# A fused two-block transformer on one core: where the last products of a gated block, the pooling bands and the pooling tiles stand, and which engine multiplies the post-norm vectors of channels 512 up

## The chip, the core and the metric

The kernel runs on one core of a Trainium2 chip. Five engines work at once, each through its own queue in the order of that queue: TensorE (PE in the profile, its weight loads PEld), VectorE (DVE), ScalarE (ACT), GpSimd (POOL), and SyncE (SP), which issues the transfers. Semaphores hold an instruction until its inputs are there; what stands behind a held instruction on the same engine waits too. The metric is the device time of one execution in microseconds.

## The reference, cut to what is computed

512 tokens of 1024 channels in float32 pass through two blocks. The first (modulated norms, a gating and convolution mixer, a gated feed-forward) is not touched. The second has two layers, an attention layer and a pooling layer, each with a gated feed-forward behind it:

```python
def second_block(h, g, ...):
    for layer in range(2):
        u = rmsnorm(h, g[layer][0])
        m = mixer_fox_nsa(u, ...) if layer == 0 else mixer_pool(u, ...)
        h = h + rmsnorm(m, g[layer][1])          # post-norm of the mixer
        u = rmsnorm(h, g[layer][2])
        h = h + rmsnorm(swiglu(u, ...), g[layer][3])   # post-norm of the feed-forward

def mixer_pool(h, w_groups, scale):      # four groups of 256 channels, windows 2, 4, 8, 16
    mean = trailing mean of the group's window of tokens
    pooled = mean - h                    # per group
    return einsum('bsgc,gcd->bsgd', pooled, w_groups) * scale
```

So four post-norms stand in the second block: attention, first gated block, pooling, second gated block. The trailing mean reaches at most 15 tokens back, so a tile of 128 tokens needs itself and the tile before it.

## The kernel before

**Tiles.** The residual `XT` is token-major: four tiles `i` of 128 tokens, each in two halves `j` of 512 channels. A product keeps float32 by three passes over operands split into a high and a low part (`wh`, `wl` of weights, `H` or `hid` of activations). A weight is loaded raw by SP, copied to `wh` on ScalarE and subtracted to `wl` on VectorE; `W.ahead(n)` asks for `n` such splits ahead of use. All engine instructions are recorded through one helper, so they carry one line, L113 before and L111 after; the tile names tell them apart.

**A post-norm** (`PostT`) has, for each token tile, per half: the mixer's or feed-forward's result is put into `mg` on VectorE (out of PSUM), `square` sums its squares on ScalarE (`sq<-mg`) and multiplies `mg` in place by the norm's vector `gb`. `TG[j]` says whether GpSimd (True) or VectorE (False) does this. `close` makes the root (`sd` on VectorE, its square root on ScalarE, the reciprocal `rs` on VectorE) and adds `mg*rs` to `XT` (two instructions `XT<-mg,rs,XT`), with two squares on ScalarE. `to_raw` then transposes `XT` on TensorE in eight products (`ax<-fixed,XT`) and puts each into `H`, high part on ScalarE, low part on VectorE: the input of the next gated block.

**First gated block** (`f2`). `front` computes all but the last 6 of the 22 hidden slabs of the down product into `mg`. `f2.last(h, j)` does the last 6 slabs for token tiles 2h and 2h+1 and half j: 18 products `mm<-wh,hid` and `mm<-wl,hid` of 128x512 for each tile, 36 in all. Behind `last(h, 1)` comes, per tile, `after2`: `close`, then `to_pool`, which writes the scaled tile as `xs` (half 0 on ScalarE, half 1 on VectorE).

**Pooling.** `band(c0, c1)` makes the pooled input of 256 tokens with banded matrices: for each of 8 channel slices it multiplies `xs` by a band (`ax<-bf,xs` and `ax<-bm,xs`, two or three products) and puts the result into `H`, 128x256, high part on ScalarE and low part on VectorE. `pool_step(i)` multiplies the four groups of tile i by their maps (48 products `mm<-wh,H` and `mm<-wl,H` for two tiles, 24 each), evacuates with `mg<-mm,gb` and does `square`, `close` and `to_raw` of the pooling post-norm.

**Second gated block** (`f3`). A "head" is one slab of 128 hidden channels, gate and up, on tokens 0 to 255: 48 products `mm<-H,wh` and `mm<-H,wl` of 128x256. There are five heads ahead of the block's `front`. Two of them, `HN3[0]`, were emitted with `late`, which holds their evacuation back.

**The order.** A scheduler places instructions on each engine's queue from program order as priority and from its own estimate of when inputs are ready; the queues are then fixed. The main sequence of the pooling layer (lines 1735 to 1754) sets the priorities; L113 is the helper `g`.

Of the kernel before, what the change touches and what calls it, by code (L numbers as in the profile page):

```python
# [32 lines left out]
HALVES = ((0, 256), (256, 512))  # L33
# [37 lines left out]
HEAD = 3  # L71
HEAD2 = 3
HEAD3 = 5
HN3 = (2, 0)
HN = (2, 1)
HNP = 8
POOLX = (2, 6)
# [15 lines left out]
B2 = ()  # L93
NB2 = 8
TAGS.update({n: ("b2", NB2) for n in B2})
LATE = 1
KEEPF = ()
KEEP = True
KEEPS = False
TG = (True, True)  # L100


class Ordered:
# [17 lines left out]
def body(ctx: ExitStack, tc: tile.TileContext, I: dict, out, dbg=None):  # L121
# [19 lines left out]
    def SQ():  # L141
        return tp.tile([P, S], F32, tag="sq", name="sq", bufs=BS)
# [13 lines left out]
    def AXP():  # L156
        return ps.tile([P, S], F32, tag="ax", name="ax", bufs=2)

    def act(o, i, f=AF.Identity, **kw):
        ins = SC.activation(o, i, f, **kw)  # L160
        if f in KEEPF and not SC.on:
            tc.keep_in_program_order(ins)
        return ins
# [269 lines left out]
    def drain(it):  # L433
        deque(it, maxlen=0)
# [453 lines left out]
    for h in range(8):  # L888
        hp, e = divmod(h, 2)
# [45 lines left out]
    def heads(n, **kw):  # L935

        for _ in range(min(n, len(nx["head"]))):
            nx["head"].popleft()(**kw)
# [80 lines left out]
    class PostT:  # L1019
# [13 lines left out]
        def square(self, i, j):  # L1033
            mv = self.m(i, j)
            act(SQ(), mv, AF.Square, accum_out=self.ss[:, i, j:j + 1])
            (G if TG[j] else V).tensor_tensor(mv, mv, self.gb[:, j], op=OP.mult)

# [606 lines left out]
    f2 = FfnT(HO, raw0, HEAD2)  # L1644
# [47 lines left out]
    def band(c0, c1):  # L1692
        i0 = c0 // P

        def xk(i, k):
            return xs[i][:, k // 4, (k % 4) * P:(k % 4 + 1) * P]

        for k in range(KD):
            lv = k // 2
            bm = bands["m"][:, lv]  # L1700
            o = AXP()[:, :HS]
            TE.matmul(o, lhsT=xk(i0, k), rhs=(bm if c0 else bands["f"][:, lv]), start=True, stop=False)
            TE.matmul(o[:, P:], lhsT=xk(i0 + 1, k), rhs=bm[:, :P], start=False, stop=(c0 == 0))
            if c0:
                TE.matmul(o[:, :16], lhsT=xk(i0 - 1, k), rhs=bm[:, P:P + 16], start=False, stop=True)
            HO.put(k, o, c0, c1, scale=ng2[:, 1, 0, k:k + 1])
# [3 lines left out]
    def pool_step(i):  # L1710
        psb, pp = pf["psb"], pf["pp"]
        for j in range(2):
            (wh, wl, _), = getp(j)
            o = MM()
            for e in range(2):
                g = 2 * j + e
                mm_tok(o[:, e * HS:(e + 1) * HS], HO, [(wh[:, 2 * e:2 * e + 2], wl[:, 2 * e:2 * e + 2], 2)], i, 2 * g)
            tt(pp.m(i, j), o, psb[:, j], OP.mult)
            pp.square(i, j)
        pp.close(i)  # L1720
        pp.to_raw(i)
# [13 lines left out]
    f2.last(0, 0)  # L1735
    f2.last(0, 1, after2)
    f2.last(1, 0)
    band(*HALVES[0])
    pool_step(0)
    pool_step(1)  # L1740
    f2.last(1, 1, after2)
    f3 = FfnT(HO, raw1, HEAD3)
    W.ahead(6)
    late = []
    heads(HN3[0], late=late)
    band(*HALVES[1])
    if LATE:
        drain(e() for e in late)
    heads(HN3[1])
    if not LATE:  # L1750
        drain(e() for e in late)
    pool_step(2)
    pool_step(3)
    heads(HEAD3)
# [26 lines left out]
```

## Time and profile before

| | us |
|---|---|
| median of 3 runs (1666.96, 1671.49, 1671.66) | 1671.49 |
| profiled execution | 1667.07 |
| span of the profiled execution, first to last instruction | 1665.3 |
| TensorE busy in it | 1627.4 |
| VectorE, ScalarE, GpSimd busy | 881.8, 681.8, 129.5 |

The profiled execution lies 4.4 us under the median. Its page gives the busy time of each engine, the chain of work that ended last, and the granted TensorE clock; the answers on its trace give, in order of time, what each engine did, how long it stood idle, and what released it. In the span's times, the stretch that the change rearranges runs from 1253.5 (end of the products of `last(1, 0)`) to 1304.7 us (end of the products of `pool_step(3)`). Before, TensorE does in it: band 0 with steps 0 and 1, `last(1, 1)` with the transposes of tiles 0 and 1 set among its products, two heads, band 1 with steps 2 and 3.

### The profile page before, as it was taken

How to read it: one execution, taken by the hardware profiler on the slowest of the kernel's cores; microseconds unless marked ns; L12 is line 12 of the kernel's file. 1: busy time of each engine (PE TensorE's matmuls, PEld its weight loads, DVE VectorE, ACT ScalarE, POOL GpSimd, SP SyncE). 2: the span in 40 equal slices, each digit the busy share in tenths (PEclk: the TensorE clock that was granted, in tenths of full speed). 3: DMA queues.
4: the chain of work that ended last, by engine and by line, in shares of the span. 5: the costliest groups of instructions: out<-in, count | busy, mean ns of one | idle time of the engine just before them, and what ended most of it. 6: DMA issues, size and time to landing. Idle time of an engine off the chain costs nothing.

```text
span 1665.3 us, 22096 instructions
## 1 busy us (share of the span) xinstructions
PE 1627.4 (98%) x8797; PEld 1358.9 (82%) x8797; DVE 881.8 (53%) x1645; ACT 681.8 (41%) x1232; POOL 129.5 (8%) x144
## 2 busy tenths in 40 slices
PE   7999899999999999999999999999999999999998
PEld 5776698887888998777778988888888998888886
DVE  5799585444333584678857344423257734432144
ACT  4585352222222364455658233213237823232232
POOL 0452000000000001100001000000013100000002
PEclk9999999999999999999999999999999999999999
DMA  9635435544531423311144232234134232232411
GB/s 306 179 111 193 152 112 175 154 149 133 153 101 54 120 57 90 90 26 52 39 107 124 61 111 61 95 114 144 59 102 114 77 89 77 83 121 93 121 64 51
DMA packets 245168, 179.55 MB, mean 108 GB/s; under 512 B 20688, under 2 KB 220224, under 8 KB 245064
## 3 DMA queue, kind: packets, MB, share of 16 engines
q1 hardware_dynamic: 240520, 176.99, 36.3%
q10 hardware_dynamic: 4544, 1.14, 0.4%
q8 instruction: 69, 1.13, 0.3%
q14 instruction: 35, 0.29, 0.1%
HBM read 175.99 MB, written 2.11 MB: 107 GB/s over the span
## 4 chain that ended last, share of the span: by engine, by line
PE 86%; DVE 3%; ACT 2%; issue 0%; DMA 0%; SPq 0%; DVEq 0%; ACTq 0%
PE mm L113 79%; PE ax L113 4%; PE st L113 3%; DVE pw L113 1%; ACT sq L113 0%; DMA raw<-in_w_out_dram 0%; ACT pw L113 0%; DVE XT L113 0%; DVE wl L113 0%; DVE sq L113 0%; ACT wh L113 0%; ACT H L113 0%; DVE pt L113 0%; DVE fk L113 0%; DVE mg L113 0%
## 5 line engine op out<-in xcount | busy, mean ns | idle before, releaser
L113 PE MATMUL mm<-H,wh 128*128 128x512 f32 (+1 forms) x3168 | 869.8, 361 | 9.2 <-ACT wh L113 3.4
L113 PEld LDWEIGHTS mm<-H,wh 128*128 128x128 f32 x3168 | 564.1, 189 | 104.5 <-issue 4.4
L113 PE MATMUL mm<-H,wl 128*128 128x512 f32 (+1 forms) x1584 | 567.7, 359 | 2.9 <-DVE wl L113 2.9
L113 DVE TENSOR_TENSOR wl<-raw,wh 128x1024 fp32r<-128x1024 f32 (+1 forms) x257 | 310.4, 1223 | 217.0 <-ACT wh L113 203.2
L113 PEld LDWEIGHTS mm<-H,wl 128*128 128x128 f32 x1584 | 299.3, 189 | 47.7 <-DVE wl L113 3.5
L113 ACT ACTIVATE wh<-raw 128x1024 fp32r<-128x1024 f32 (+1 forms) x257 | 262.5, 1041 | 127.3 <-PE mm L113 52.8
L113 PE MATMUL mm<-wh,hid 128*128 128x512 f32 x704 | 217.3, 389 | 0.0
L113 DVE TENSOR_TENSOR silu<-silu,mm 128x512 f32<-128x512 f32 (+1 forms) x77 | 47.0, 611 | 250.0 <-PE mm L113 243.5
L113 PEld LDWEIGHTS mm<-wh,hid 128*128 128x128 f32 x704 | 132.1, 188 | 27.1
L113 ACT ACTIVATE hid<-silu 128x512 fp32r<-128x512 f32 (+1 forms) x77 | 43.8, 569 | 242.5 <-DVE silu L113 234.9
L113 PE MATMUL mm<-wl,hid 128*128 128x512 f32 x352 | 137.3, 390 | 0.0
L113 PE MATMUL mm<-hid,wh 128*128 128x512 f32 (+1 forms) x464 | 116.4, 340 | 0.0
L113 PEld LDWEIGHTS mm<-hid,wh 128*128 128x128 f32 x464 | 80.3, 190 | 9.9 <-issue 0.4
L113 POOL TENSOR_TENSOR mg<-mg,gb 128x512 f32<-128x512 f32 x32 | 44.3, 1389 | 464.6 <-ACT sq L113 456.0
L113 ACT ACTIVATE silu<-silu 128x512 f32<-128x512 f32 (+1 forms) x52 | 29.3, 565 | 123.1 <-DVE silu L113 123.0
L113 PE MATMUL mm<-hid,wl 128*128 128x512 f32 (+1 forms) x232 | 79.1, 341 | 0.0
L113 PEld LDWEIGHTS mm<-wl,hid 128*128 128x128 f32 x352 | 66.1, 188 | 14.0 <-DVE wl L113 0.3
L113 DVE TENSOR_TENSOR silu<-mm,rsb 128x512 f32<-128x512 f32 (+1 forms) x52 | 31.6, 608 | 73.0 <-PE mm L113 72.5
L113 PE MATMUL mm<-wh,H 128*128 128x512 f32 (+2 forms) x256 | 67.0, 350 | 1.6 <-ACT wh L113 1.6
L113 DVE TENSOR_TENSOR hid<-silu,hid 128x512 fp32r<-128x512 f32 (+1 forms) x77 | 47.3, 614 | 37.4 <-ACT hid L113 37.3
L113 POOL TENSOR_TENSOR cv<-cv,tap 128x488 f32<-128x488 f32 (+12 forms) x40 | 52.5, 1348 | 88.2 <-ACT cv L113 71.2
L113 ACT ACTIVATE silu<-mm 128x512 f32<-128x512 f32 (+1 forms) x25 | 13.7, 546 | 108.7 <-PE mm L113 108.7
(271 smaller groups left out, 1624.7 us busy)
## 6 DMA issues: line engine op xcount, KB each, us to landing
adaw<-in_ada_w_dram SPq DMA_DIRECT2D x48, 512.0 KB
raw<-in_w_ffn_in_dram SPq DMA_DIRECT2D x44, 512.0 KB
raw<-in_ffn_w_gate_dram SPq DMA_DIRECT2D x44, 512.0 KB
raw<-in_ffn_w_up_dram SPq DMA_DIRECT2D x44, 512.0 KB
raw<-in_ffn_w_down_dram SPq DMA_DIRECT2D x44, 512.0 KB
raw<-in_w_in_dram SPq DMA_DIRECT2D x16, 512.0 KB
adaw<-in_ada_f_w_dram SPq DMA_DIRECT2D x16, 512.0 KB
raw<-in_attn_w_in_dram SPq DMA_DIRECT2D x16, 512.0 KB
```

The lines of the kernel that those rows point to most:

```text
L113: ins = f(*a, **k)
```

## The change

`HN3` and `LATE` go. `f2.last(1, 1)` moves ahead of band 0, so all of the first gated block's last products precede both bands. Band 1 follows pooling steps 0 and 1; then come the construction of `f3`, `W.ahead(6)`, steps 2 and 3, and all five heads together. `TG` becomes `(True, False)`: the in-place product with the post-norm vector for channels 512 up goes to VectorE in every post-norm of the second block, 16 of the 32 instructions `mg<-mg,gb`.

```diff
-HN3 = (2, 0)
-LATE = 1
-TG = (True, True)
+TG = (True, False)
...
     f2.last(0, 1, after2)
     f2.last(1, 0)
+    f2.last(1, 1, after2)
     band(*HALVES[0])
     pool_step(0)
     pool_step(1)
-    f2.last(1, 1, after2)
+    band(*HALVES[1])
     f3 = FfnT(HO, raw1, HEAD3)
     W.ahead(6)
-    late = []
-    heads(HN3[0], late=late)
-    band(*HALVES[1])
-    if LATE:
-        drain(e() for e in late)
-    heads(HN3[1])
-    if not LATE:
-        drain(e() for e in late)
     pool_step(2)
     pool_step(3)
     heads(HEAD3)
```

**TensorE behind the products of pooling step 1.** Before, the last products of `last(1, 1)` stand there, with the transposes of tile 0 among them:

```order
L113 MATMUL mm<-wh,H_97 128x256 x2
L113 MATMUL mm<-wl,H_97 128x256
L113 MATMUL mm<-wh,hid 128x512 x2
L113 MATMUL mm<-wl,hid 128x512
L113 MATMUL mm<-wh,hid 128x512
L113 MATMUL ax<-fixed,XT 128x128 x4
L113 MATMUL mm<-wh,hid 128x512
L113 MATMUL ax<-fixed,XT 128x128 x4
L113 MATMUL mm<-wl,hid 128x512
```

After, the transposes stand there by themselves, nine, one small product, seven, and band 1 stands behind them:

```order
L111 MATMUL mm<-wh,H_97 128x256 x2
L111 MATMUL mm<-wl,H_97 128x256
L111 MATMUL ax<-fixed,XT 128x128 x9
L111 MATMUL st<-fixed 128x128
L111 MATMUL ax<-fixed,XT 128x128 x7
L111 MATMUL ax<-bm,xs 128x256
L111 MATMUL ax<-bm,xs 128x128
L111 MATMUL ax<-bm,xs 128x16
L111 MATMUL mm<-wh,H_90 128x256
L111 MATMUL ax<-bm,xs 128x256
```

What moved is `last(1, 1)`, now in front of band 0; all sixteen transposes of tiles 0 and 1 follow step 1 directly, and every product of band 1 is behind them.

**VectorE from the last put of band 0 to the residual of tile 0.** `wl` is a weight split, `mg<-mm,gb` the evacuation of a pooling product, `XT<-mg,rs,XT` the residual that the transposes wait for. Before:

```order
L113 SCALAR_TENSOR_TENSOR H_97<-ax,fixed,H_97 128x256
L113 TENSOR_TENSOR mg<-mm,gb 128x512 x2
L113 TENSOR_TENSOR wl<-raw,wh 128x1024
L113 TENSOR_TENSOR sd<-fixed 128x1
L113 TENSOR_TENSOR mg<-mm,gb 128x512
L113 RECIPROCAL rs<-sd 128x1
L113 SCALAR_TENSOR_TENSOR XT<-mg,rs,XT 128x512 x2
```

After:

```order
L111 SCALAR_TENSOR_TENSOR H_97<-ax,fixed,H_97 128x256
L111 RECIPROCAL rs<-sd 128x1
L111 TENSOR_SCALAR xs<-XT,rs 128x512
L111 TENSOR_TENSOR wl<-raw,wh 128x1024 x3
L111 TENSOR_TENSOR mg<-mm,gb 128x512 x2
L111 TENSOR_TENSOR wl<-raw,wh 128x1024
L111 TENSOR_TENSOR mg<-mm,gb 128x512
L111 TENSOR_TENSOR mg<-mg,gb 128x512
L111 TENSOR_TENSOR sd<-fixed 128x1
L111 TENSOR_TENSOR mg<-mm,gb 128x512
L111 RECIPROCAL rs<-sd 128x1
L111 TENSOR_TENSOR wl<-raw,wh 128x1024
L111 SCALAR_TENSOR_TENSOR XT<-mg,rs,XT 128x512 x2
```

Behind the last put there is now the `xs` of tile 3, then three splits in a row ahead of the first evacuation, one more between the evacuations of tiles 0 and 1, and one ahead of tile 0's residual; ScalarE's queue has the `wh` copies of the same weights there, four in a row. The three splits stood among the band's puts before, ahead of the first evacuation; a fourth stood behind it. One of tile 1's two evacuations stood ahead of tile 0's residual before; now both do, and a product `mg<-mg,gb` too.

**VectorE at the end of the program**, the post-norm of the last tile's channels 512 up. Before:

```order
L113 TENSOR_TENSOR mg<-mg,mm 128x512
L113 TENSOR_TENSOR sd<-fixed 128x1
L113 RECIPROCAL rs<-sd 128x1
L113 TENSOR_TENSOR rs<-rs,fixed 128x1
L113 SCALAR_TENSOR_TENSOR XT<-mg,rs,XT 128x512 x2
```

After:

```order
L111 TENSOR_TENSOR mg<-mg,mm 128x512
L111 TENSOR_TENSOR mg<-mg,gb 128x512
L111 TENSOR_TENSOR sd<-fixed 128x1
L111 RECIPROCAL rs<-sd 128x1
L111 TENSOR_TENSOR rs<-rs,fixed 128x1
L111 SCALAR_TENSOR_TENSOR XT<-mg,rs,XT 128x512 x2
```

The product with the vector stands on VectorE between the last addition to `mg` and the root; before it stood on GpSimd. In the other three post-norms it enters in the same way; the attention's post-norm is the third place where TensorE's order differs (the transposes of `XT` stand elsewhere among the output products).

## Rows read from the trace of the kernel before

**Rows 1.** the page: busy time by engine, and the chain that ended last

```profile
PE 1627.4 (98%) x8797; PEld 1358.9 (82%) x8797; DVE 881.8 (53%) x1645; ACT 681.8 (41%) x1232; POOL 129.5 (8%) x144
...
PE 86%; DVE 3%; ACT 2%; issue 0%; DMA 0%; SPq 0%; DVEq 0%; ACTq 0%
```

**Rows 2.** TensorE in time order: start, us, instruction, count, [idle before <-releaser]

```profile
1252.79 0.61 PE L113 MATMUL mm<-wh,hid 128*128 128x512 f32 x2
1253.24 0.39 PE L113 MATMUL mm<-wl,hid 128*128 128x512 f32 x1
1253.47 1.46 PE L113 MATMUL ax<-bf,xs 128*128 128x256 f32 x6
1256.93 1.42 PE L113 MATMUL ax<-bm,xs 128*128 128x128 f32 x6 [2.00 <-ACT xs L113]
...
1262.21 0.60 PE L113 MATMUL ax<-bf,xs 128*128 128x256 f32 x2
...
1262.86 0.60 PE L113 MATMUL ax<-bf,xs 128*128 128x256 f32 x2
...
1265.55 0.40 PE L113 MATMUL mm<-wh,H 128*128 128x256 f32 x2
...
1268.43 0.63 PE L113 MATMUL mm<-wh,hid 128*128 128x512 f32 x2
...
1270.66 0.63 PE L113 MATMUL ax<-fixed,XT 128*128 128x128 f32 x4 [1.14 <-DVE XT L113]
...
1280.02 0.40 PE L113 MATMUL mm<-H,wh 128*128 128x256 f32 x2
...
1291.89 4.46 PE L113 MATMUL ax<-bm,xs 128*128 128x256 f32 x30
...
1304.68 0.40 PE L113 MATMUL mm<-H,wh 128*128 128x256 f32 x2
```

**Rows 3.** windows of 2 us: busy by engine, then granted clock, DMA share, GB/s

```profile
1256.00:1258.00 2.00, 1.07 (x6) 1.10 (x6) 0.83 (x2) 1.94 (x4) 1.72 (x2) 0.79 0.49 143
1258.00:1260.00 2.00, 2.00 (x8) 1.73 (x8) 2.00 (x4) 1.17 (x4) 0.00 (x0) 0.50 1.16 315
1260.00:1262.00 2.00, 2.00 (x14) 1.81 (x13) 1.39 (x3) 1.99 (x4) 0.00 (x0) 0.86 1.16 290
```

**Rows 4.** VectorE in time order, same stretch

```profile
1257.76 1.22 DVE L113 TENSOR_TENSOR wl<-raw,wh 128x1024 fp32r<-128x1024 f32 x1 [1.17 <-ACT wh L113]
1258.90 1.26 DVE L113 SCALAR_TENSOR_TENSOR H<-ax,fixed,H 128x256 fp32r<-128x256 f32 x3
...
1265.02 1.43 DVE L113 TENSOR_TENSOR mg<-mm,gb 128x512 f32<-128x512 f32 x2
...
1279.20 0.61 DVE L113 SCALAR_TENSOR_TENSOR H<-ax,fixed,H 128x128 fp32r<-128x128 f32 x2
```

**Rows 5.** ScalarE in time order, same stretch

```profile
1250.44 0.72 ACT L113 ACTIVATE xs<-XT,rs 128x512 f32<-128x512 f32 x1 [0.30 <-DVE rs L113]
...
1256.69 1.04 ACT L113 ACTIVATE wh<-raw 128x1024 fp32r<-128x1024 f32 x1
```

**Rows 6.** waits of TensorE between 862 and 918 us

```profile
PE ax L113 <- DVE XT L113: 0.2, 1, 0.2
```

**Rows 7.** all engines in time order at the end

```profile
1657.45 0.39 PE L113 MATMUL mm<-wl,hid 128*128 128x512 f32 x1
...
1658.05 0.68 DVE L113 TENSOR_TENSOR mg<-mg,mm 128x512 f32<-128x512 f32 x1
...
1659.56 1.26 POOL L113 TENSOR_TENSOR mg<-mg,gb 128x512 f32<-128x512 f32 x1 [2.96 <-ACT sq L113]
...
1660.33 0.51 DVE L113 TENSOR_TENSOR rs<-rs,fixed 128x1 f32<-128x1 f32 x1
1660.88 1.42 DVE L113 SCALAR_TENSOR_TENSOR XT<-mg,rs,XT 128x512 f32<-128x512 f32 x2
```

**Rows 8.** VectorE in time order, some 20 us before the end

```profile
1640.85 0.16 DVE L113 TENSOR_TENSOR rs<-rs,fixed 128x1 f32<-128x1 f32 x1
```

## The prediction

> **What bounds the kernel now.** I read the page first: TensorE is busy 98% of the span and makes 86% of the chain that ended last [rows 1]. So a microsecond that TensorE waits is a microsecond of the kernel, and one of another engine counts only where TensorE then waits for it. Next I read TensorE in order of time where the change works [rows 2]. Two waits stand there: 2.00 us behind the first bands, until ScalarE has written the last `xs` of tile 1, and 1.14 us until VectorE has written `XT` of tile 0. Behind the first the granted clock falls: in 2 us windows 0.79, 0.50 and 0.86 [rows 3]. Full speed is 1.00, and 0.50 is the lower level (1.2 of 2.4 GHz), so the low time is 2 x (0.21 + 0.50 + 0.14)/0.50 = 3.4 us, and half of it, 1.7 us, is lost. From 1280.02 to 1304.68 no row shows a wait. The reader should see what covers the close of each pooling tile (evacuation, squares, root, residual, before TensorE can transpose): the 36 products of `last(1, 1)`, 8.2 us of work that needs nothing from it.
>
> **The change, the move of the last products.** I follow the queue of after with durations of before, from a common start at 1253.47, where `last(1, 0)` ends.
>
> Step 1. `last(1, 1)` now comes at once: 36 products, three in 0.68 us (1252.79 to 1253.47, [rows 2]), 8.2 us, to 1261.6. The `xs` of tile 1 are written meanwhile, so the 2.00 us wait, its 1.7 us of low clock and the 1.14 us wait go: 4.8 us.
>
> Step 2. Band 0 costs 0.65 us a slice (1262.21 to 1262.86, [rows 2]), eight make 5.2; step 0's 24 products at 0.12 us (step 1 takes 1265.55 to 1268.43) make 2.9: 1269.7. But the band's puts into `H` now share VectorE with the closes of tiles 2 and 3 of the first gated block: 8 puts of 0.42, a `mg` addition and a vector product of 0.7 each, two residuals of 0.7 [rows 4, 7], an `xs` at about 0.7 (as ScalarE's, [rows 5]) and six short ones of 0.16 [rows 8], in all 7.9 us, and some 1.5 us for which it waits on ScalarE's squares and roots between. From 1261.6 this ends the last put at about 1271.0. Step 0 then ends at 1271.2 (1.5 us lost) and step 1 at 1274.1.
>
> Step 3. Now the transposes of tile 0 stand next in TensorE's queue, and nothing is in front of them. VectorE's queue from 1271.0: three splits, paced by ScalarE's root (some 0.3), `xs` (0.7) and three copies (1.04 each), with a last `wl` of 1.22 [rows 4, 5]: 5.3 us, to 1276.3. Then two evacuations, a split, an evacuation, the product with the vector, the sum for the root, an evacuation while ScalarE makes the root, the reciprocal, a fifth split and the first half of tile 0's residual: six of 0.7, two of 1.2 and two of 0.16 make 6.9 us, less some 0.4, since an instruction in a row starts about 0.08 before the one ahead ends (1258.90 behind 1257.76 + 1.22, [rows 4]). TensorE gets it at 1282.8 and has waited 8.7 us. The five splits alone are 5 x 1.2 = 6 us of this.
>
> Step 4. Tile 1. Behind tile 0's residual stand a sixth split (1.2), eight low puts of 0.3 that alternate with ScalarE's high puts, a vector product (0.7), roots and the two residuals: 5.1 us of work besides the split, and some 1.3 us on ScalarE. That ends at 1291.0; the last transposes at 1291.4. From 1274.1 to there TensorE has 1.5 us of work, so it waits 15.8 us.
>
> Step 5. Band 1 with steps 2 and 3 is the same work as before, 1291.89 to 1304.68, 12.8 us. Its first products after the band wait for puts that now stand behind those of tile 1 on ScalarE and VectorE: from their queue I put 1.9 us. The clock: the 2.00 us wait above cost 1.7 us of low clock, and this wait is longer, so it costs that at least; I take 1.7, the row it is nearest to. If it stayed low through all of band 1 and steps 2 and 3, it would cost 12.8. End: 1291.4 + 12.8 + 1.9 + 1.7 = 1307.8.
>
> Step 6. The two heads that stood at 1280.02 to 1291.89, 11.9 us, now come behind: 1319.7, where before had done the same work at 1304.68. The transposes of tiles 2 and 3 stand among the heads' products, five times 48 at 0.12 us, some 29 us of other work, and cost no wait. The rest of TensorE's queue is as before. So the move costs **15.0 us**.
>
> **The vector product on VectorE.** 16 products of about 0.7 us (the `mg` evacuation, [rows 4]) leave GpSimd, where one takes 1.26 [rows 7]. In the pooling tiles they are in the sum. In the attention's post-norm TensorE waits 0.2 us in 56 us [rows 6]; with a product of 0.7 for each of four tiles ahead of roots that transposes wait for, it can grow by 1.5 at most if two such delays show, or by nothing; I take 0.5. At the second gated block all closes but the last lie beside products. At the end of the program the chain from the last product (1657.84) to the residual (1662.30) is 4.46 us and nothing covers it [rows 7]: the product adds 0.7. But the small `rs` product takes 0.51 us while GpSimd runs and 0.16 where it does not [rows 7, 8], so 0.35 comes back: +0.3, with 0 and 0.7 as bounds. By these rows an instruction of VectorE that meets one of GpSimd is the longer for it.
> The Trainium skill's Perfetto Trace Analysis, Optimizing Scalar/DVE Operations, says that GpSimd and VectorE share a read port, so that moving work between the two might not help. By that alone the move to VectorE would be worth nothing at the end instead of +0.3; the trace agrees that they hinder each other, and the order puts the product on the chain all the same.
>
> **The rivals.** *Short closes.* The splits may hardly hold VectorE, because their weights arrived early and they fit into its pauses during band 0. Then each close is as short as at the end of the program: 4.46 us from the last product. Step 0 ends at 1271.2, so tile 0's residual is there at 1275.7; step 1 ends at 1274.1, tile 1's at 1278.6, transposes to 1279.0. That is 12.4 us less than step 4's 1291.4, and the sum is 15.0 - 12.4 + 0.8 = +3.4: 1675, no change that can be told. For it: before, the first three splits do lie among the band's puts. Against it: in the new order they stand behind the last put and the `xs`, and a queue doesn't reorder; the three ahead of the evacuations and two behind are 6 us. It decides at about 10 us taken out of steps 3 and 4.
>
> *The removed waits win.* If besides the puts of step 2 and the `H` of step 5 came in time (1.5 and 1.9 us less), and the short waits left the clock high (1.7 less), the sum were 3.4 - 5.1 = -1.7, and with tile 1's close as well beside tile 0's transposes at most -5: 1666 to 1670, on the other side. The place is TensorE's wait behind step 1, the price 8.7 and 7 us in the forecast; it decides where both closes together show under 3 us. The 4.46 us at the end, with nothing else on VectorE, speaks against it.
>
> *Slower still.* The clock stays low through band 1 and steps 2 and 3: up to 11.1 more than in step 5, +27: 1698. For it: there are two waits, of 8.7 and 7 us, with few products between, four times the one that made the clock fall before. Against it: after that one the clock was full again within 3.4 us of low time [rows 3]. Late weights would act in the same way: in 1258 to 1262 the transfers run at 290 to 315 GB/s [rows 3], so 3 MB of loads take 10 us, and copies that wait for them hold VectorE's splits and all behind them.
> The Trainium skill's TensorE: Matmul & The Clock Gate, HAM oscillation, reckons the loss of a low stretch as its length times a half. The 1.7 us above follow that already; by it a low stretch twice as long after the long wait would cost 3.4 instead of 1.7, and the sum +17.4.
>
> **How the numbers follow.** 15.0 + 0.5 + 0.3 = +15.8 us. On the profiled execution's own 1667.07 that is 1682.9; on the median, 4.4 above it, 1687.3. I forecast **1687**. Chances: forecast 0.72, short closes 0.09, removed waits 0.04, slower still 0.15. A measurement can tell about 0.3%, 5 us, from no change. Faster by more has 0.03 and within 0.3% 0.10 (of the removed waits 0.01 lies within 5 us), slower 0.87. The forecast's own bounds: steps 3 and 4 rest on an order that is fixed, but their waits on ScalarE (1.5, 1.3 and 1.9) may be nothing or double, and the base is 1667 or 1671.5: from 1667.1 + 15.8 - 6 = 1677 to 1671.5 + 15.8 + 5 = 1692. For 8 in 10 it reaches some way to the cases at both sides: 1674 to 1697.
>
> **What would show it.** Right: in the changed profile TensorE waits for `XT` from VectorE some 8 us behind step 1 and again 5 to 7 us for tile 1; neither of the waits of 2.00 and 1.14 us is there; the granted clock reads 0.5 behind these waits; VectorE shows three splits between the last put and the first evacuation. Wrong: if TensorE's waits in the stretch come to under 10 us in all; if the splits lie before 1271; if there are further waits among the five heads; or if the time is lost where TensorE's order has not changed.

## The result, and the profile after

The changed kernel takes 1680.66 us (median of 6, 1677.47 to 1683.52) against 1670.14 us of the kernel before run beside it: a ratio of 1.0066, 95% interval 1.005 to 1.0082, or some 11 us slower. The forecast was 1687, +15.8, in a range of 1674 to 1697.

The profiled execution takes 1682.4 us, 15.3 more than the one of before. The page answers [rows 1]: TensorE is as busy as before, its share has fallen, since the span grew and the work did not.

```profile
PE 1630.0 (97%) x8797; PEld 1361.4 (81%) x8797; DVE 887.8 (53%) x1661; ACT 681.7 (41%) x1232; POOL 107.7 (6%) x128
...
PE 85%; DVE 4%; ACT 2%; issue 1%; DMA 0%; SPq 0%; DVEq 0%; ACTq 0%
```

To compare stretches I use one distance in every trace: from the end of the products of `last(1, 0)` to the start of the last product of the program. Before it is 1657.45 - 1253.47 = 404.0 us [rows 2, 7]. In after, band 0 starts at 1263.43 behind `last(1, 1)`, whose 36 products take 8.16, so the start is 1255.27 and the distance 1672.19 - 1255.27 = 416.9: **+12.9 us**. The end behind it grew by 0.6. The other 1.8 us lie ahead of 1253.5, where 2.3 stand already at the start of the attention's output products (851.44 before, 853.71 after), in code that is the same in both: scatter of single executions, not the change. The distance comes from single executions, too: the one of before lies 3.1 us under its median and the one of after 1.7 above, while the medians differ by 10.5 us and the ratio makes 11. Where distance and ratio differ, the ratio decides.

This is TensorE in order of time, answering [rows 2]:

```profile
1263.43 0.59 PE L111 MATMUL ax<-bf,xs 128*128 128x256 f32 x2
...
1267.06 0.38 PE L111 MATMUL mm<-wh,H 128*128 128x256 f32 x1 [0.49 <-ACT H L111]
...
1275.22 0.28 PE L111 MATMUL mm<-wl,H 128*128 128x256 f32 x1
1284.07 1.94 PE L111 MATMUL ax<-fixed,XT 128*128 128x128 f32 x8 [8.57 <-DVE XT L111]
1290.67 0.48 PE L111 MATMUL ax<-fixed,XT 128*128 128x128 f32 x1 [4.66 <-DVE XT L111]
...
1291.59 1.70 PE L111 MATMUL ax<-fixed,XT 128*128 128x128 f32 x7
1293.08 1.49 PE L111 MATMUL ax<-bm,xs 128*128 128x256 f32 x6
1295.23 0.39 PE L111 MATMUL mm<-wh,H 128*128 128x256 f32 x1 [0.66 <-ACT H L111]
...
1307.33 0.28 PE L111 MATMUL mm<-wl,H 128*128 128x256 f32 x1
```

The waits of 2.00 and 1.14 us are gone, and the 36 products do stand in front of band 0. Behind step 1's last product (1275.22) TensorE waits 8.57 us for the residual of tile 0 and, eight transposes later, 4.66 us for that of tile 1. The windows show the granted clock, third from the end of a row, as in [rows 3]:

```profile
1278.00:1280.00 2.00, 0.00 (x0) 0.00 (x0) 2.00 (x3) 1.93 (x6) 0.80 (x1) 1.00 0.00 0
1280.00:1282.00 2.00, 0.00 (x0) 0.00 (x0) 2.00 (x5) 1.10 (x2) 0.84 (x1) 0.63 0.00 0
1282.00:1284.00 2.00, 0.00 (x0) 0.00 (x0) 2.00 (x5) 0.66 (x1) 0.00 (x0) 0.50 0.00 0
...
1292.00:1294.00 2.00, 2.00 (x10) 1.82 (x9) 0.71 (x3) 1.58 (x6) 0.00 (x0) 0.50 0.00 0
1294.00:1296.00 2.00, 1.34 (x10) 1.19 (x9) 1.81 (x7) 1.53 (x6) 0.00 (x0) 0.96 0.00 0
```

It falls at about 1280.5, while TensorE stands idle, is at the lower level (0.50, 1.2 of 2.4 GHz) for tile 0's and tile 1's transposes, and is full again from about 1294.2. Why TensorE waits is read on VectorE, which answers [rows 4]:

```profile
1273.87 3.50 DVE L111 TENSOR_TENSOR wl<-raw,wh 128x1024 fp32r<-128x1024 f32 x3 [1.22 <-ACT wh L111]
1277.29 1.28 DVE L111 TENSOR_TENSOR mg<-mm,gb 128x512 f32<-128x512 f32 x2
1278.49 1.23 DVE L111 TENSOR_TENSOR wl<-raw,wh 128x1024 fp32r<-128x1024 f32 x1
1279.63 0.68 DVE L111 TENSOR_TENSOR mg<-mm,gb 128x512 f32<-128x512 f32 x1
1280.23 1.16 DVE L111 TENSOR_TENSOR mg<-mg,gb 128x512 f32<-128x512 f32 x1
...
1282.06 1.20 DVE L111 TENSOR_TENSOR wl<-raw,wh 128x1024 fp32r<-128x1024 f32 x1
1283.18 1.40 DVE L111 SCALAR_TENSOR_TENSOR XT<-mg,rs,XT 128x512 f32<-128x512 f32 x2
...
1290.87 0.73 DVE L111 SCALAR_TENSOR_TENSOR XT<-mg,rs,XT 128x512 f32<-128x512 f32 x1
```

There are the three splits behind the last `xs`, the two evacuations behind them, a split, an evacuation, the product with the vector, a split, and then the residual at 1283.18. From 1275.3 to 1285.3 VectorE is busy for the whole 10 us; it is TensorE that idles. The product `mg<-mg,gb` at 1280.23 took 1.16 us; the median of the 16 is 0.69. GpSimd multiplies its half of the same tile from 1279.20 to 1280.84.

### The profile page after: what moved, and what is told of

It is laid out like the page before. It is cut to its first block, busy times and chain, and to the rows that moved or that the text cites. A ratio compares the mean times of both kernels' runs of the same rounds, so it can differ in the third digit from the quotient of the medians.

```text
span 1680.7 us, 22087 instructions
## 1 busy us (share of the span) xinstructions
PE 1630.0 (97%) x8797; PEld 1361.4 (81%) x8797; DVE 887.8 (53%) x1661; ACT 681.7 (41%) x1232; POOL 107.7 (6%) x128
## 3 DMA queue, kind: packets, MB, share of 16 engines
q10 hardware_dynamic: 4544, 1.14, 0.4%
## 4 chain that ended last, share of the span: by engine, by line
PE 85%; DVE 4%; ACT 2%; issue 1%; DMA 0%; SPq 0%; DVEq 0%; ACTq 0%
PE mm L111 79%; PE ax L111 3%; PE st L111 3%; DVE pw L111 1%; ACT sq L111 1%; DVE mg L111 0%; DVE wl L111 0%; DMA raw<-in_w_out_dram 0%; ACT pw L111 0%; ACT H L111 0%; DVE H L111 0%; DVE XT L111 0%; DVE sq L111 0%; ACT wh L111 0%; DVE pt L111 0%
## 5 line engine op out<-in xcount | busy, mean ns | idle before, releaser
L111 ACT ACTIVATE silu<-mm 128x512 f32<-128x512 f32 (+1 forms) x25 | 13.7, 546 | 110.2 <-PE mm L111 110.2
L111 POOL TENSOR_TENSOR mg<-mg,gb 128x512 f32<-128x512 f32 x16 | 22.5, 1408 | 466.8 <-ACT sq L111 445.5
```

The costliest lines, as they stand in the source:

```text
L111: ins = f(*a, **k)
```

## The experiments

All runs were compared with the kernel before on their own chip. "Distance" is the one above, in the profiled execution.

| run | ratio to before | interval | distance against before, us | waits of TensorE from 1240 to 1345, us | work lost to the low clock from 1250 to 1350, us |
|---|---|---|---|---|---|
| before | 1 | | 0 | 3.1 | 1.7 |
| after | 1.0066 | 1.005 to 1.0082 | +12.9 | 14.4 | 2.7 |
| e1, vector product alone | 0.9992 | 0.9982 to 1.0002 | +2.1 | 3.9 | 1.7 |
| e2, order alone | 1.007 | 1.0056 to 1.0085 | +13.6 | 12.0 | 5.1 |
| e8, move of the last products alone | 1.0064 | 1.0047 to 1.008 | +10.1 | 11.0 | 2.8 |
| e9, heads behind alone | 1.0088 | 1.007 to 1.0106 | +15.5 | 13.0 | 6.3 |
| e3, after without splits | 1.005 | 1.0033 to 1.0067 | +9.0 | 10.0 | 2.6 |
| e4, both bands first | 1.0029 | 1.0017 to 1.004 | +5.6 | 6.9 | 2.7 |
| e5, later transposes | 1.0029 | 1.0019 to 1.0039 | +7.4 | 4.7 | 5.0 |
| e6, both bands first, no splits | 1.0017 | 1.0006 to 1.0028 | +4.2 | 5.0 | 3.0 |
| e7, later transposes, no splits | 1.0015 | 1.0002 to 1.0028 | +4.3 | 4.9 | 3.2 |
| e10, last products by tiles | 1.0035 | 1.0022 to 1.0048 | +7.0 | 9.1 | 3.1 |

The last column is worked out from windows of 1 us: the time that TensorE worked in each, times the share of full speed that the granted clock lacked. Waits and lost work together, less the 4.8 us of before, give each distance to within 1.4 us (e5: 2.5 us), and the ratio as well (1670 us times what it has over 1) to within 2.2 us. So no third cause of more than that size is needed.

**Which part of the change? e1 and e2.** e1 is the kernel before with the other `TG`; e2 is after with the old one.

```diff
-TG = (True, True)
+TG = (True, False)
```

> The order of the kernel before, with the vector product of channels 512 up on VectorE alone. Theory (the move of the last products makes the loss, by TensorE's uncovered closes): TensorE's queue is all but the old one, so the change is small: +0.3 us at the end, at most some +1 in the pooling closes; ratio 1.000 to 1.001, and TensorE's waits between the last products of the first gated block and the end of pooling step 3 stay at about 3 us. Rival 1 (the product on VectorE lengthens every close and is the cause): a ratio of 1.004 or more, with waits for XT of several us there.

> The order of after, with all vector products on GpSimd again. Theory: nearly the whole loss is here, +9 to +13 us, ratio 1.005 to 1.008, with two waits for XT behind step 1 of about 8 and 4 us and the low clock behind them; the end is 4.5 us from the last product to the last residual again. Rival 1: under +4 us, ratio below 1.0025.

e1 can't be told from before. Of its waits of TensorE, here by cause with the sum, the number and the longest, the two old ones are 0.3 and 0.5 us shorter; 1.3 us on puts are new, of which 0.74 stand among the heads, and so does a wait of 0.3 for a small product that is not shown:

```profile
PE ax L113 <- ACT xs L113: 1.7, 1, 1.7
PE mm L113 <- ACT H L113: 1.3, 3, 0.7
PE ax L113 <- DVE XT L113: 0.6, 1, 0.6
```

e2 carries the whole loss. Rival 1 falls: sixteen products more on VectorE cost nothing that shows. A part of my expectation for e2 failed: its waits for XT are 4.85 and 3.38 us, not 8 and 4. There four of the band's puts stand behind the last `xs`, one split among them and two behind, so steps 0 and 1 wait 2.2 us for puts (1.55, 0.25 and 0.43) and tile 0 is awaited for less; and the clock is low for longer (0.50 in 1280 to 1290 and 0.69 in 1290 to 1300, so to 1296.2), with 5.1 us of work lost to it instead of 2.7. The ratio is the same.

**Which part of the order? e8 and e9.** e8 moves `last(1, 1)` and leaves the heads:

```diff
     f2.last(1, 0)
+    f2.last(1, 1, after2)
     band(*HALVES[0])
     pool_step(0)
     pool_step(1)
-    f2.last(1, 1, after2)
```

e9 moves the heads behind steps 2 and 3 and leaves `last(1, 1)`:

```diff
     f2.last(1, 1, after2)
+    band(*HALVES[1])
     f3 = FfnT(HO, raw1, HEAD3)
     W.ahead(6)
-    late = []
-    heads(HN3[0], late=late)
-    band(*HALVES[1])
...
-    heads(HN3[1])
...
     pool_step(2)
```

> The kernel before, and of the change only the move of the last products ahead of band 0; the two heads stay between the steps and band 1, the vector products on GpSimd. Theory (closes of tiles 0 and 1 lose their cover, and heads can't give any since they read those tiles): two waits for XT behind step 1 of 8 to 12 us in all, and the low clock; the stretch 7 to 13 us longer, ratio 1.004 to 1.008. Rival: it is the missing heads between the bands that cost; then this run is within 3 us of before.

> The kernel before, and of the change only the place of the heads: band 1 directly behind the last products, steps 2 and 3, then all five heads. Theory: band 1 now stands behind last products and transposes with nothing to cover the close of tile 3 (xs some 5 us behind the last product), so one wait for xs of 3 to 6 us and a low clock behind it: 5 to 8 us, ratio 1.003 to 1.005. Rival: this part alone costs as much as the whole change, 10 us and more.

Each part alone costs about as much as both, or more: they don't add. The rival of e8, that the missing heads are what costs, falls. In e8 TensorE waits 2.2 us for puts in steps 0 and 1, as in e2, and then for tiles 0 and 1 behind step 1:

```profile
1285.45 1.94 PE L113 MATMUL ax<-fixed,XT 128*128 128x128 f32 x8 [4.84 <-DVE XT L113]
1290.78 2.04 PE L113 MATMUL ax<-fixed,XT 128*128 128x128 f32 x8 [3.38 <-DVE XT L113]
```

In e9 the old cover is kept for tiles 0 and 1, but nothing stands between the last products and band 1. TensorE waits for a small product of tile 1's norm (`st`), and twice for `xs`:

```profile
1286.23 0.49 PE L113 MATMUL st<-fixed 128*128 128x128 f32 x2 [3.14 <-DVE fixed L113]
1289.44 2.93 PE L113 MATMUL ax<-bm,xs 128*128 128x256 f32 x6 [2.72 <-ACT xs L113]
1294.22 2.74 PE L113 MATMUL ax<-bm,xs 128*128 128x128 f32 x12 [1.85 <-ACT xs L113]
```

The clock behind them is low for 10 us:

```profile
1290.00:1300.00 10.00, 8.15 (x29) 6.77 (x28) 6.60 (x14) 6.23 (x13) 0.00 (x0) 0.50 0.36 106
```

I expected 5 to 8 us of e9; it is 15, and the rival, that this part alone costs 10 us and more, held. The waits for `xs` are 4.6 us, as expected (3 to 6). What I had not counted is the 3.1 us for the norm, which the heads had covered too, and a clock that stays low for 10 us, of which TensorE worked 8.15 at half speed: some 4 us. Another 2 us are small waits, half of them among the heads. So cover is what both moves take away: the last products cover the close of tiles 0 and 1, the two heads that of tiles 2 and 3. When all is moved, as in after, band 1 comes behind waits in which the closes of tiles 2 and 3 are long done, and the heads' absence costs nothing more.

**What is in the wait? e3.** The splits are taken out from between the pooling tiles and follow ahead of the heads.

```diff
     f2.last(1, 1, after2)
+    W.look = 0
     band(*HALVES[0])
...
-    W.ahead(6)
     pool_step(2)
     pool_step(3)
+    W.look = 4
+    W.ahead(6)
     heads(HEAD3)
```

> After, with the look-ahead of weights set to nothing through the pooling tiles, so that no split stands on VectorE between the last xs and tile 1's residual; the same splits follow ahead of the heads. Theory (the five splits and their copies are 6 of the 8.6 us wait behind step 1): the first wait falls from 8.6 to about 2.5 to 3.5 us (the close alone: 4.46 us from the end of step 0, less step 1's 2.9, plus the evacuations in common), the second from 4.7 to about 4; some 7 us less in the stretch, ratio to before about 1.003, unless the heads then wait for weights, which would show as waits for wh or wl among them. Rival 2 (the chain of evacuation, squares and root itself takes the time, and the splits lie in its pauses): the first wait stays over 6 us.

```profile
1279.01 1.94 PE L111 MATMUL ax<-fixed,XT 128*128 128x128 f32 x8 [2.19 <-DVE XT L111]
1285.62 0.80 PE L111 MATMUL st<-fixed 128*128 128x128 f32 x2 [4.67 <-DVE fixed L111]
...
1304.36 0.38 PE L111 MATMUL mm<-H,wl 128*128 128x256 f32 x1 [0.91 <-DVE wl L111]
```

The first wait falls from 8.57 to 2.19, so the splits, with their copies on ScalarE, were 6.4 us of it, as step 3 had it (6). Rival 2 falls. But the second wait stays: 4.67 us for a small product of tile 0's norm, whose root VectorE makes just ahead of tile 1's residual, and 0.16 for that, against 4.66. The low clock stays too, and the heads now wait 1.7 us for weights in two waits (0.91 is one): of 6.4 us the distance shows 3.9. The intervals of e3 and after overlap, so the gain in time is not shown for certain; the shorter wait is.

**Is it cover? e4.** Band 1 is asked for ahead of steps 0 and 1, so 12.8 us of products stand ahead of the transposes.

```diff
     band(*HALVES[0])
+    band(*HALVES[1])
     pool_step(0)
     pool_step(1)
-    band(*HALVES[1])
```

> After, with band 1 asked for ahead of pooling steps 0 and 1, so that band 1's and steps 2 and 3's products, 12.8 us, stand between step 1 and the transposes of tiles 0 and 1. Theory (the loss is missing cover, not work): the waits for XT fall from 13.2 to under 2 us, the clock does not fall, the stretch is 13 to 16 us shorter than in after and 0 to 4 shorter than before; ratio to before 0.997 to 1.001. Rival 3 (the work on VectorE and ScalarE bounds this stretch, in whatever order): the waits only move, to puts of band 1 or to the heads, and the ratio stays at 1.004 or more.

More than half of the loss is gone, and tile 0's transposes wait for nothing. Tile 1's still do:

```profile
1290.90 0.63 PE L111 MATMUL ax<-fixed,XT 128*128 128x128 f32 x4
...
1297.84 0.80 PE L111 MATMUL st<-fixed 128*128 128x128 f32 x2 [5.47 <-DVE rs L111]
1299.22 1.97 PE L111 MATMUL ax<-fixed,XT 128*128 128x128 f32 x8 [0.58 <-DVE XT L111]
```

They wait 5.5 us at the small product of tile 0's norm ahead of them and 0.58 for the residual itself. This is three times what my theory allowed, and the clock fell again (0.85 in 1290 to 1300). VectorE shows what is ahead of tile 1's residual (1298.42):

```profile
1285.91 1.22 DVE L111 TENSOR_TENSOR wl<-raw,wh 128x1024 fp32r<-128x1024 f32 x1
1287.04 1.78 DVE L111 TENSOR_TENSOR mg<-mg,gb 128x512 f32<-128x512 f32 x1
...
1291.39 1.22 DVE L111 TENSOR_TENSOR wl<-raw,wh 128x1024 fp32r<-128x1024 f32 x1
...
1295.97 1.23 DVE L111 TENSOR_TENSOR wl<-raw,wh 128x1024 fp32r<-128x1024 f32 x1
...
1298.42 1.41 DVE L111 SCALAR_TENSOR_TENSOR XT<-mg,rs,XT 128x512 f32<-128x512 f32 x2
```

Three splits, a product that took 1.78 us beside one of GpSimd, and the puts of tile 0 between. From 1280 to 1300 VectorE is busy 17.8 of 20 us. So cover is one cause, and what VectorE has to do in the stretch a second one, as rival 3 had it in part.

**Both causes together: e5, e6, e7.** e5 is after with the transposes of tiles 0 and 1 asked for later, e6 is e4 without splits, e7 is e5 without splits (the edit of e3).

```diff
         pp.close(i)
-        pp.to_raw(i)
+        if i > 1:
+            if i == 2:
+                pp.to_raw(0)
+                pp.to_raw(1)
+            pp.to_raw(i)
```

> After, with only the transposes of tiles 0 and 1 and their puts asked for later, behind the products of pooling step 2; bands and splits as in after. TensorE's queue then has band 1 and most of steps 2 and 3 between step 1 and these transposes, and VectorE has no puts of tile 0 ahead of tile 1's residual. Theory (the place of the transposes in TensorE's queue is what uncovers the closes, and tile 0's puts hold tile 1's residual): waits for XT and st under 2 us in all, no low clock behind them, ratio to before 0.997 to 1.001. Rival 3 (the work of VectorE in this stretch, splits included, is the bound in whatever order): 5 us and more of waits turn up further on, as in the run with both bands first, where 6 us were left; ratio 1.002 to 1.004.

> Both bands first, as in that run, and the six splits taken out from between the bands and the heads. Rival 3 in its sharper form (cover is there now, and what is left of 6 us is VectorE's load, 7 us of it splits): the wait of 5.5 us for tile 1 falls under 1 us, and the ratio from 1.003 to 0.998 to 1.000, unless the heads then wait for weights, which shows as waits for wh or wl. Theory that tile 0's puts alone hold tile 1: the wait stays at 4 us or more.

> The later transposes and the splits taken out, together. If cover and VectorE's load are the two causes and nothing else is, TensorE shows no wait over 1 us in the stretch until the heads, and the gain of the removed waits of the old order (2.0 and 1.1 us and 1.7 us of low clock) is seen at last: 3 to 5 us under before, ratio 0.997 to 0.998, less what the heads wait for weights.

e5 does about what e4 does: its waits come to 4.7 us, in eight places with 1.2 the longest, and the ratio is the same, about as rival 3 said. The theory's waits are as short as it had them (1.7 us for `XT` and `st`, under 2), but its clock is not: 0.86, 0.84 and 0.79 in the three stretches of 10 us from 1280 to 1310, that is low for 10.2 us, nearly all of it with TensorE at work, and 5.0 us lost. e6 takes the waits for tile 0's norm and tile 1 from 5.5 and 0.6 to 1.78 and 1.46, not under 1:

```profile
1293.59 0.46 PE L111 MATMUL st<-fixed 128*128 128x128 f32 x2 [1.78 <-DVE rs L111]
1295.50 1.94 PE L111 MATMUL ax<-fixed,XT 128*128 128x128 f32 x8 [1.46 <-DVE XT L111]
```

e7 has a wait of 2.34 us among the transposes, where I expected none over 1, and one in the heads for a split, and the granted clock (third from the end of a row) falls behind each:

```profile
1291.74 1.11 PE L111 MATMUL ax<-fixed,XT 128*128 128x128 f32 x4 [2.34 <-DVE H L111]
...
1297.14 0.39 PE L111 MATMUL mm<-H,wl 128*128 128x256 f32 x1 [1.79 <-DVE wl L111]
...
1290.00:1300.00 10.00, 6.47 (x33) 6.00 (x34) 9.13 (x31) 9.05 (x29) 1.99 (x1) 0.74 0.49 133
1300.00:1310.00 10.00, 10.00 (x79) 9.91 (x79) 8.50 (x20) 8.51 (x20) 0.00 (x0) 0.92 1.16 296
```

It is the nearest to before of all that keep the moved products, 1.0015, and still not under it. The 4.8 us of removed waits and low clock are seen in none of them, since others came in their place: in e7 4.9 us of waits and 3.2 us lost to the clock, 8.1 in all. Taking the splits out brings 1.2 to 1.4 thousandths by the middles of intervals that overlap; part of the wait goes on to the heads.

**Half of each? e10.** The last products of tile 2 stand ahead of band 0, those of tile 3 behind step 1.

```diff
     f2.last(1, 0)
+    f2.last(1, 1, after2, (2,))
     band(*HALVES[0])
     pool_step(0)
     pool_step(1)
-    f2.last(1, 1, after2)
+    f2.last(1, 1, after2, (3,))
```

> The kernel before, with the last products of tile 2 ahead of band 0 and those of tile 3 behind step 1: 4.1 us of cover for each of the two closes. If cover is all that counts, the 2.0 us wait and its 1.7 us of low clock go, and the wait for XT behind step 1 grows by 4.1 us less the splits' change: -4 to +4 us, ratio 0.998 to 1.002. If VectorE's load counts, the wait behind step 1 is over 6 us and the ratio 1.002 or more.

```profile
1276.82 1.94 PE L113 MATMUL ax<-fixed,XT 128*128 128x128 f32 x8 [5.64 <-DVE XT L113]
1282.23 2.04 PE L113 MATMUL ax<-fixed,XT 128*128 128x128 f32 x8 [3.47 <-DVE XT L113]
```

The wait of 2.0 us went, as it should, and the waits behind step 1 came to 9.1 us instead of 1.1: 4.1 us less of cover cost 8.0 us of waits. Cover alone does not decide; the second case of the expectation held (over 6 us, 1.002 or more). VectorE has a split ahead of tile 0's evacuations here, too (1268.55, 1.22 us), and a last addition and a split (1271.82, 1.80 us) between them and its root.

No run beats the kernel before by more than its interval; e1 comes nearest.

## Why the prediction was right, point by point

**The bound and the place** held: the loss is TensorE's, in the stretch that the order showed, and where the order is the same nothing changed. The wait for `xs` went, the wait for tile 0 moved behind step 1 and grew, and the clock did not fall behind `last(1, 0)`.

**Step 1**: 8.16 us for the last products, as forecast.

**Step 2**: forecast 1.5 us of waits for band 0's puts; 0.49 measured (1267.06). The end of step 1 is at 1275.50, 20.2 us behind the start, where 20.6 were forecast.

**Step 3**: the first wait was forecast at 8.7 us and is 8.57; e3 gives the splits 6.4 us of it, forecast 6. The queue was read rightly: VectorE's order, followed with durations of the trace before, gave the wait to 0.2 us.

**Step 4**: the second wait was forecast at 15.8 - 8.7 = 7.1 us and is 4.66, just under the 5 that was to show the forecast right. Half of the difference is a real miss: the residual of tile 1 is there at 1291.60, 36.3 us behind the start, where 37.5 were forecast. Of these 1.2 us steps 2 and 3 bring 0.5, and the rest is in the main the alternation of ScalarE's and VectorE's puts: I had added 1.3 us of waiting, and VectorE shows two waits there, 0.52 and 0.26 us (1286.78, 1287.64). The other half is time that I had put down as wait and that TensorE spent on tile 0's transposes at the low clock (8 took 1.94 us).

**Step 5** was mis-sized: 1.9 us of waits for band 1's puts, 0.66 measured (1295.23). The clock came out at what I took: low to 1294.2, of which 2.4 us for tile 1's transposes and 1.1 us of band 1 lie on the path, half of them lost: 1.7 us. That is not a half of the low stretch: the clock was low for 13.7 us, TensorE worked in 5.4 of them and lost 2.7, of which 1.0 lies in tile 0's transposes, ahead of a wait that would have come anyway. That it would stay low through band 1 and steps 2 and 3 did not happen in after. From 1293.08 to the end of step 3 (1307.45) are 14.4 us, forecast 16.4.

**Step 6** and the sum: +12.9 instead of +15.0 in the distance: 1.2 us up to tile 1's residual and 1.2 at band 1's puts, less 0.3 of small ones. By the medians the forecast was half too large, 15.8 against 10.5 us: the place and the mechanism were right, the size was not. 1687 lies 6 us above the measured median: 1.4 us of this is its base (1671.49 instead of 1670.14), 2.1 are these terms, and the rest lies in the main between the profiled executions and the medians. No wait stands among the five heads, as forecast. The step that was mis-sized is the same each time: hand-offs between ScalarE and VectorE that I added to a queue's work by judgement, 1.5, 1.3 and 1.9 us. Where I had only added up a queue (step 3) the sum held.

**The vector product**: forecast +0.8 in all; its two parts measure +0.2, and e1 shows no loss. Forecast +0.5 at the attention; there is no wait there now, and from 851.44 to 934.95 us before and from 853.71 to 936.80 after are 83.5 and 83.1 us: -0.4. At the end forecast +0.3; measured +0.6 (4.46 to 5.06 us from the last product to the residual):

```profile
1671.75 1.42 DVE L111 SCALAR_TENSOR_TENSOR XT<-mg,rs,XT 128x512 f32<-128x512 f32 x2
...
1672.19 0.39 PE L111 MATMUL mm<-wl,hid 128*128 128x512 f32 x1
...
1673.08 0.68 DVE L111 TENSOR_TENSOR mg<-mg,mm 128x512 f32<-128x512 f32 x1
...
1674.55 0.69 DVE L111 TENSOR_TENSOR mg<-mg,gb 128x512 f32<-128x512 f32 x1 [0.79 <-ACT sq L111]
...
1675.97 0.16 DVE L111 TENSOR_TENSOR rs<-rs,fixed 128x1 f32<-128x1 f32 x1
1676.23 1.41 DVE L111 SCALAR_TENSOR_TENSOR XT<-mg,rs,XT 128x512 f32<-128x512 f32 x2
```

The product adds 0.6 and the short `rs` step gives 0.29 back, as forecast. The 0.3 more is the step I left out: the last addition (1673.08) now waits for the residual of the tile ahead (1671.75 + 1.42), which the same product had delayed. e1 has 5.08 and e2 the old 4.46. The Trainium skill's Perfetto Trace Analysis (Optimizing Scalar/DVE Operations) says that moving work between the two engines might not help; over the whole program e1 agrees with it (0.9992), at the end the move costs 0.6 us. That whatever VectorE does beside GpSimd takes longer, as I had read from one row, is too wide; the last section has what the runs show.

**The rivals**: *short closes* was wrong as a whole, but e3 shows that its condition was the right one: without the splits the first wait is 2.19 us. Its second half, that tile 1 would then follow at once, is not borne out: 4.8 us remain. *The removed waits win* was wrong, and e7 shows more against it than I had: even with cover and without splits they don't win. *Slower still* did not happen here, though e9 shows its mechanism at work, with the clock at 0.50 for 10 us.

**What stays open**: whether an order exists in which the 4.8 us come out. In e6 and e7 some 3 us remain by the ratio (2.8 and 2.5), and the table says where: 1.8 to 1.9 us more of waits than before and 1.3 to 1.5 us more lost to the low clock behind them. VectorE is busy 8.3 of 10 us through the 60 us behind the start in e7, 9.7 from 1294.3 to 1304.3, and TensorE's waits there are for splits and puts. That less work on VectorE alone would remove them is argued, not shown.

## What to carry to other kernels

When products are moved ahead to fill one wait, look for the close that they covered where they stood: here they filled waits of 2.0 and 1.1 us and uncovered two closes. Follow the queue of the engine that makes the close, not the close alone: three quarters of the first new wait (6.4 of 8.57 us) were weight splits that a scheduler had put ahead of it, on an engine that is busy only half of the span. And test the parts of a reordering one by one: by the ratios these two cost 11 and 15 us alone and 11 together. Count the clock with the waits: in e5 4.7 us of short waits came with 5.0 us lost to the low clock.

## What the runs showed of the hardware

A product of 128x512 on VectorE, 0.69 us by the median, took 1.16 us (after) and 1.78 us (e4) where GpSimd multiplied at the same time, more than the 0.35 us that I had read from the small `rs` step. The two rows of VectorE behind 1279.63 above, beside this row of GpSimd, show more:

```profile
1279.20 1.64 POOL L111 TENSOR_TENSOR mg<-mg,gb 128x512 f32<-128x512 f32 x1 [19.49 <-issue]
```

The evacuation `mg<-mm,gb`, which reads one operand out of PSUM, ran inside it in its usual 0.68 us; the product `mg<-mg,gb`, which reads both out of SBUF, ended 0.55 us behind GpSimd's end at 1280.84, as it would if it stood still until then. Over the profiles of all twelve kernels, each of the 19 such products that began beside one of GpSimd ended 0.55 us behind it, and each of the 22 evacuations that began so took 0.67 to 0.69. A close's small sum `sd`, 0.15 us alone, was held in the same way: 1.25 us in before (1267.50). So the products on GpSimd cost VectorE time in the closes as well, which fits that e1 costs nothing; no run separates the two.

The granted clock of after fell during the first wait (idle from 1275.50, low from about 1280.5), stayed low through tile 0's eight transposes and the second wait, and was full again at 1294.2, behind 3.5 us of transposes and band products. In e9 it was at 0.50 from 1290 to 1300 although TensorE was busy for 8.15 of those 10 us.
